# Layer A attention of a decoder trunk: the TensorE order written out, keys transposed two blocks later, the stages of a unit two and four steps apart, and the query root on POOL

## The chip, the cores and the metric

The kernel runs on one core of one Trainium2 chip. The metric is the device time of one execution in microseconds. The kernel before took 2514.96 us (median of 3 runs, 2512.82 to 2516.09). The engines are named as in the profile: PE is TensorE (matmuls and transposes), DVE is VectorE, ACT is ScalarE, POOL is GpSimd, SP is SyncE, which here issues DMAs. Each engine takes its own instructions strictly in the order in which they stand in its queue.

## The reference

The program is a trunk of four sub-layer pairs on x of 1024 rows by 1024 columns: layer A, a feed-forward block, layer B (stick-breaking attention), a feed-forward block. The change touches layer A alone, which computes

```
qkv = h @ w_qkv                              # h: normed, scaled and shifted x
q = rope(rmsnorm(q, q_gain)); k = rope(rmsnorm(k, k_gain))   # per head of 64
# 16 query heads in 2 groups of 8, one key/value head for each group
# for each block of 128 queries: keys of its own and of the block before
s = q @ k.T * 64 ** -0.5                      # 0 <= query - key < 128
p = softmax(concat(s, sink))[..., :-1]        # one sink logit for each head
x = x + gate * ((p @ v) @ w_o)
```

The rope turns only the first 16 of a head's 64 columns. The sums must come out in full fp32, while TensorE's fast format (fp32r) rounds its operands. So an operand is split into a rounded high part and a low part, the rest, and a product is made of three matmuls: high by high, high by low and low by high.

## The kernel before

The rows are cut into 8 blocks of 128. First `keys_values(b)` makes keys and values of block b: 24 matmuls of 256 columns (3 for each of 8 slices of the sum), a copy to `kvf` by ACT, the root of two heads (`head_rms`), gain and rope on POOL, the high and low part side by side in `kd`, and then four transposes of `kd` on PE (L461) and their copy into `KTs` (L462). The input norm comes in two halves of four blocks: `norm_half` (L474) turns the second half into `hth` and `htl`, the high and low part of h, between the keys of block 3 and of block 4.

Then come 16 units (g, b): head group g of 8 query heads, block b. A unit has three stages.

- `stage1`: the query projection, 24 matmuls of 512 columns into one PSUM bank `psd`; its product with the gain, `qn` (DVE, L490); the squares `sq` (ACT, L407), their sum (DVE, L409) and the root of 8 heads by three Newton steps, 12 small DVE instructions (L416 to L422); the rope on POOL, five small instructions (L430 to L434); the high part of `qs` (ACT, L495) and its low part (POOL, L496).
- `stage2`: 8 transposes of `qs` (PE, L505) in two halves, each copied into `QT` (ACT, L506); four times 4 matmuls of 256 columns, the scores `psz`, whose diagonal blocks ACT copies into `sm` (L520) and whose other half DVE puts in above the diagonal (L524); the maximum `mx` and the bias `nmx` (DVE, L525 to L532); 8 exponentials, one for each head (ACT, L535); the sum, its reciprocal and the product `sm` (DVE, L536 to L538).
- `stage3`, for each half of the heads: 4 transposes of `sm`, its high part `ph` (ACT, L548) and low part `pl` (DVE, L119); two selections `ow` of them on POOL (L559); 4 matmuls of 512 columns into the bank `psa` with the values; the copy `ob` (ACT, L563) and its DMA to DRAM.

The loop (L581 to L602) goes through steps t and traces `stage2` of unit t-1, `stage3` of unit t-3 and `stage1` of unit t, so the text of a step holds three units. Beside them stand weight work (the query weights of group 1, loaded at t = 8, with a high part on ACT and a low part on DVE; the output weights `W`, from t = 12 on), one `ada_step` a step (a slice of the next scale and shift row, DVE L268, and at t = 9 eight matmuls with `ones` and two with `diag`, L297, that make the gate row `grow`, L302), and behind the loop the output projection, which reads the units back from DRAM.

A tile scheduler orders the instructions of each engine by its own estimate of when they are ready. `chained` (L99 to L105) can tie each matmul to the one traced before it, so that TensorE's order becomes the written one; before the change this is off in layer A.

Of the kernel before, what the change touches and what calls it, by code (L numbers as in the profile page):

```python
# [18 lines left out]
P = 128  # L19
# [45 lines left out]
def build(tc, x_in, c_in, pos_in, ada_w, ada_b, n1g, n2g, wqkv_a, qn_a, kn_a, sinks, wo_a,  # L65
# [338 lines left out]
    def head_rms(src, nh, pool):  # L404
# [34 lines left out]
    def keys_values(b):  # L439
# [14 lines left out]
        kd = kt.tile([P, 2, 2, 2, HD], F32R, tag="kd", name=nm("kd"), bufs=2)  # L454
# [3 lines left out]
        pt = bank("t", F32R)  # L458
        kdf = kd.rearrange("p v e u d -> p (v e) (u d)")
        for j in range(4):  # L460
            chained(nc.tensor.transpose(pt[:, j * P : (j + 1) * P], kdf[:, j], identr))  # L461
        nc.scalar.copy(KTs[:, :, b * P : (b + 1) * P], pt.rearrange("p (j t) -> p j t", t=P))  # L462
# [20 lines left out]
    def stage1(g, b, wq):  # L483
        pb = bank("d")
        for k in range(KT):
            h, l = hA_blk(b, k)
            wh, wl = wq[k // 2]
            mm3(pb, h, l, wh[:, k % 2], wl[:, k % 2], k == 0, k == KT - 1)
# [5 lines left out]
        qs = wk.tile([P, 8, 2, HD], F32R, tag="qs", name=nm("qs"), bufs=2)  # L494
# [4 lines left out]
    def stage2(g, b, qs, r):  # L499
        QT = wk.tile([P, 8, P], F32R, tag="QT", name=nm("QT"), bufs=2)  # L500
        qsf = qs.rearrange("p h e d -> p h (e d)")
        for j in range(2):
            pt = bank("t", F32R)
            for h in range(4):
                chained(nc.tensor.transpose(pt[:, h * P : (h + 1) * P], qsf[:, 4 * j + h], identr))  # L505
            nc.scalar.copy(QT[:, 4 * j : 4 * j + 4], pt.rearrange("p (h t) -> p h t", t=P))  # L506
        sm = wk.tile([P, 8, P], F32, tag="sm", name=nm("sm"), bufs=3)
# [4 lines left out]
        for j in range(4):  # L512
# [26 lines left out]
        return sm  # L539

    def stage3(g, b, sm):
        for j in range(2):
# [6 lines left out]
            sub(pl, pt, ph)  # L549
            av = bank("a")  # L550
# [31 lines left out]
    for t in range(len(units) + 3):  # L582
# [5 lines left out]
        if t < len(units):  # L588
            g, b = units[t]
            if b == 0:  # L590
                with tc.issue_after(last_norm.ins):
                    wq[g] = load_q(g)
# [639 lines left out]
```

## Time and profile before

| | |
|---|---|
| median of 3 runs | 2514.96 us (2512.82 to 2516.09) |
| the profiled execution, its own time | 2506.01 us |
| its span in the profile | 2504.3 us |
| mean granted TensorE clock | 0.976 of full speed |
| busy: PE / DVE / ACT / POOL | 2359.5 / 1604.8 / 1036.6 / 646.4 us |

The span is the time from the first to the last instruction of the profiled execution. A granted clock of 1.00 is TensorE's 2.4 GHz level, and a stretch in which the mean lies between 0.5 and 1.00 was spent partly at the 1.2 GHz level. Busy time is the share in which an engine had work in hand. A TensorE row's duration is the time that one instruction takes from start to end; since matmuls are pipelined, what one costs in a dense stream is the distance of two starts.

### The profile page before, as it was taken

To read this page: it belongs to the slowest core of one execution; us is meant where nothing else is said; L and a number is where in the kernel's file an instruction comes from. 1 tells how busy PE (TensorE), PEld (TensorE's weight loads), DVE (VectorE), ACT (ScalarE), POOL (GpSimd) and SP (SyncE) were. 2 spreads that over 40 slices of the span, in tenths; PEclk is the share of its full clock that TensorE was granted. 3 is DMA by queue.
4 is the path that set the end of the run, shared out by engine and by line. 5 is a ranking of instruction groups with operands and counts; after the bars stand their busy time and mean duration, and the time that the engine had idled before them with its cause. 6 is when DMAs were issued, how large, how long until landed. Compare 5 with 4: busy or idle time off the path is not lost.

```text
span 2504.3 us, 31440 instructions
## 1 busy us (share of the span) xinstructions
PE 2359.5 (94%) x11404; PEld 1934.1 (77%) x11404; DVE 1604.8 (64%) x2319; ACT 1036.6 (41%) x2029; POOL 646.4 (26%) x671
## 2 busy tenths in 40 slices
PE   6899899799999999999999999988979999999999
PEld 5677677578787878887788888777758888887887
DVE  7679955765767677536677676696375454557553
ACT  4487723423232332104666666573343333323110
POOL 2344512223232300001444444341212322310000
PEclk9799899899999999999999999999989999999999
DMA  8113398143536264203222222127522222227211
GB/s 288 51 50 120 110 228 249 62 130 122 175 120 182 95 238 143 82 9 101 70 58 60 60 56 53 41 80 168 143 76 74 82 93 68 91 86 257 84 51 68
DMA packets 187195, 273.78 MB, mean 109 GB/s; under 512 B 11792, under 2 KB 131744, under 8 KB 187040
## 3 DMA queue, kind: packets, MB, share of 16 engines
q1 hardware_dynamic: 186416, 271.63, 35.2%
q8 instruction: 90, 1.47, 0.2%
q14 instruction: 65, 0.53, 0.1%
q10 hardware_dynamic: 624, 0.14, 0.0%
HBM read 206.72 MB, written 56.62 MB: 105 GB/s over the span
## 4 chain that ended last, share of the span: by engine, by line
PE 70%; DVE 9%; DMA 4%; issue 2%; ACT 2%; POOL 1%; SPq 0%; DVEq 0%; ACTq 0%; POOLq 0%
PE psz L108 24%; PE psd L108 21%; PE pst L108 16%; PE psa L108 5%; DMA ada<-in_ada_w_dram 2%; PE pst L116 2%; DVE nb L1101 2%; DVE acc L268 1%; DVE al L119 1%; DVE lT L119 1%; DVE Wl L309 0%; DMA wr<-in_wo_b_dram 0%; DVE QK L119 0%; DVE sl L631 0%; ACT nb L1094 0%
## 5 line engine op out<-in xcount | busy, mean ns | idle before, releaser
L630 ACT CAST sh<-rg 128x512 fp32r<-128x512 f32 x308 | 191.5, 622 | 565.6 <-PE psz L108 246.1
L631 DVE TENSOR_TENSOR sl<-rg,sh 128x512 fp32r<-128x512 f32 x308 | 244.8, 795 | 94.0 <-ACT sh L630 94.0
L108 PE MATMUL psd<-hth,whl 128*128 128x512 f32 x768 | 304.3, 415 | 0.1
L1103 POOL TENSOR_TENSOR bb<-bb,nb 128x895 f32<-128x895 f32 (+7 forms) x128 | 179.1, 1402 | 248.7 <-DVE nb L1101 159.5
L1101 DVE TENSOR_TENSOR_SCAN nb<-nb,ones 128x896 f32<-128x896 f32 (+7 forms) x128 | 192.4, 1508 | 44.3 <-ACT nb L1094 41.9
L308 ACT CAST dh<-raw 128x1024 fp32r<-128x1024 f32 x88 | 87.9, 1048 | 277.8 <-PE psa L108 174.9
L803 POOL TENSOR_TENSOR rg<-rg,rg 128x512 f32<-128x512 f32 x44 | 58.3, 1324 | 459.8 <-DMA rg<-in_w_up_dram 361.0
L108 PEld LDWEIGHTS psd<-hth,whl 128*128 128x128 f32 x768 | 146.5, 191 | 22.2 <-issue 1.3
L108 PE MATMUL psz<-hT,sh 128*128 128x512 f32 x352 | 139.5, 399 | 19.0 <-ACT hT L684 10.8
L108 PE MATMUL psd<-htl,whl 128*128 128x512 f32 x384 | 152.3, 399 | 1.8 <-DVE htl L119 1.6
L119 DVE TENSOR_TENSOR al<-pst,ah 128x512 fp32r<-128x512 f32 x160 | 108.3, 684 | 62.1 <-ACT ah L1124 59.5
L108 PE MATMUL psz<-lT,sh 128*128 128x512 f32 x352 | 140.0, 398 | 2.7 <-DVE lT L119 2.7
L108 PE MATMUL psz<-hT,sl 128*128 128x512 f32 x352 | 139.0, 395 | 0.0
L108 PE MATMUL psd<-hB,sl 128*128 128x512 f32 x352 | 137.4, 390 | 0.0
L108 PE MATMUL psd<-hB,sh 128*128 128x512 f32 x352 | 137.3, 390 | 0.0
L108 PE MATMUL psd<-lB,sh 128*128 128x512 f32 x352 | 137.0, 389 | 0.0
L268 DVE SCALAR_TENSOR_TENSOR acc<-ada,condT,acc 128x1024 f32<-128x1024 f32 x77 | 111.0, 1441 | 25.5 <-DMA ada<-in_ada_w_dram 24.8
L1094 ACT ACTIVATE nb<-psz 128x448 f32<-128x448 f32 (+3 forms) x192 | 95.3, 496 | 65.6 <-PE psz L108 61.3
L1124 ACT CAST ah<-pst 128x512 fp32r<-128x512 f32 x160 | 94.2, 591 | 54.1 <-PE pst L116 51.8
L309 DVE TENSOR_TENSOR dl<-raw,dh 128x1024 fp32r<-128x1024 f32 x88 | 104.6, 1220 | 9.8 <-ACT dh L308 9.8
L108 PE MATMUL psz<-QK,QK 128*128 128x384 f32 (+4 forms) x384 | 104.7, 356 | 2.5 <-ACT bb L1095 2.4
L108 PE MATMUL psa<-al,V 128*128 128x256 f32 x320 | 88.9, 299 | 17.5 <-DVE al L119 16.7
(325 smaller groups left out, 6336.8 us busy)
## 6 DMA issues: line engine op xcount, KB each, us to landing
ada<-in_ada_w_dram SPq DMA_DIRECT2D x96, 512.0 KB, 4.6
rg<-in_w_gate_dram SPq DMA_DIRECT2D x44, 512.0 KB, 3.6
rg<-in_w_up_dram SPq DMA_DIRECT2D x44, 512.0 KB, 5.7
raw<-hid SPq DMA_DIRECT2D x44, 512.0 KB, 6.6
raw<-in_w_down_dram SPq DMA_DIRECT2D x44, 512.0 KB, 4.4
hid<-f SPq DMA_DIRECT2D x64, 256.0 KB, 2.1
wr<-in_wqkv_b_dram SPq DMA_DIRECT2D x24, 512.0 KB, 4.2
odA<-ob SPq DMA_DIRECT2D x32, 256.0 KB, 2.5
```

The source lines that it names most:

```text
L108: chained(nc.tensor.matmul(o, l, r, start=start, stop=stop, skip_group_check=more))
L119: return nc.vector.tensor_tensor(o, a, h.bitcast(F32), op=ALU.subtract)
L268: i = nc.vector.scalar_tensor_tensor(a, wt, condT[:, j : j + 1], a, op0=ALU.mult, op1=ALU.add)
L308: nc.scalar.copy(h, raw)
L309: (eng or nc.vector).tensor_tensor(l, raw, h.bitcast(F32), op=ALU.subtract)
L630: nc.scalar.copy(hv, src)
L631: nc.vector.tensor_tensor(lv, src, hv.bitcast(F32), op=ALU.subtract)
L803: nc.gpsimd.tensor_tensor(A[1, 0], A[1, 0], A[1, 1], op=ALU.add)
L1094: nc.scalar.activation(nb[:, s0 : s0 + e], pz[:, 0:e], AF.Sigmoid, scale=-1.0)
L1101: nc.vector.tensor_tensor_scan(rv, rv, ones[:, 0:1].to_broadcast([P, L]), initial=1.0, op0=ALU.mult, op1=ALU.mult)
L1103: nc.gpsimd.tensor_tensor(bb[:, 0 : L - 1], bb[:, 0 : L - 1], nb[:, 1:L], op=ALU.mult)
L1124: nc.scalar.copy(ah_, pt)
```

## The change

- `head_rms` makes the root of 8 heads as it did that of 2: an addition and a power on POOL in place of the 12 small DVE instructions.
- `keys_values` no longer transposes. `keys_turned(b)` does, two blocks later, and `kd` has three buffers.
- TensorE's order is the traced one from the keys and values of block 0 up to the last query projection (`pe["on"]`).
- The first two query projections stand right behind the keys of block 7. From t = 2 on, a step weaves three streams of TensorE work: the projection of unit t in 8 parts, `stage2` of unit t-2 in 6 parts and `stage3` of unit t-4 in 4 parts. The rest of `stage1` (gain, root, rope, `qs`) is traced at the end of the step. `qs` has three buffers.
- In `stage3` both halves are transposed and split first, and the selections `ow` of a half are issued ahead of the matmuls of the half before. `ob` is written over `sm`, in place of a tile of its own.

```diff
@@ head_rms
-        if nh <= 2:
-            nc.gpsimd.tensor_scalar(r, r, EPS, None, op0=ALU.add)
-            nc.gpsimd.tensor_tensor(r, r, mhalf[:, 0:nh], op=ALU.pow)
-        else:
...
-            nc.vector.tensor_scalar(v, r, EPS, None, op0=ALU.add)
-            nc.vector.tensor_scalar(r.bitcast(I32), v.bitcast(I32), 1, None, op0=ALU.logical_shift_right)
-            nc.vector.tensor_scalar(r.bitcast(I32), r.bitcast(I32), -1, 0x5F3759DF, op0=ALU.mult, op1=ALU.add)
-            for _ in range(3):
-                nc.vector.tensor_tensor(t, r, r, op=ALU.mult)
-                nc.vector.scalar_tensor_tensor(t, v, -0.5, t, op0=ALU.mult, op1=ALU.mult)
-                nc.vector.scalar_tensor_tensor(r, t, 1.5, r, op0=ALU.add, op1=ALU.mult)
+        nc.gpsimd.tensor_scalar(r, r, EPS, None, op0=ALU.add)
+        nc.gpsimd.tensor_tensor(r, r, mhalf[:, 0:nh], op=ALU.pow)
@@ keys_values
-        kd = kt.tile([P, 2, 2, 2, HD], F32R, tag="kd", name=nm("kd"), bufs=2)
+        kd = kt.tile([P, 2, 2, 2, HD], F32R, tag="kd", name=nm("kd"), bufs=3)
...
+    def keys_turned(b, kd):
+        pt = bank("t", F32R)
+        kdf = kd.rearrange("p v e u d -> p (v e) (u d)")
+        for j in range(4):
+            chained(nc.tensor.transpose(pt[:, j * P : (j + 1) * P], kdf[:, j], identr))
+        nc.scalar.copy(KTs[:, :, b * P : (b + 1) * P], pt.rearrange("p (j t) -> p j t", t=P))
...
+    def proj_q(g, b, wq):
+        pb = bank("d")
+        q_banks[g, b] = pb
+        for k in range(KT):
+            h, l = hA_blk(b, k)
+            wh, wl = wq[k // 2]
+            mm3(pb, h, l, wh[:, k % 2], wl[:, k % 2], k == 0, k == KT - 1)
+            yield
+    pe["on"] = True
     for b in range(4):
-        keys_values(b)
-    norm_half(xta, xA, 0, adaT[:, 0, 0], *HA[1], True)
+        kd[b] = keys_values(b)
+        if b >= 2:
+            keys_turned(b - 2, kd[b - 2])
+    xns = norm_rows(xta, xA, True)
+    for kk in range(KT):
+        norm_cols(xns, kk, xA, 0, adaT[:, 0, 0], *HA[1])
+        if kk in (3, 7):
+            b = 2 + kk // 4
+            keys_turned(b, kd[b])
+    with tc.issue_after(last_norm.ins):
+        wq[0] = load_q(0)
     for b in range(4, NB):
-        keys_values(b)
+        kd[b] = keys_values(b)
+        if b >= 6:
+            keys_turned(b - 2, kd[b - 2])
+    for b in range(2):
+        for _ in proj_q(0, b, wq[0]):
+            pass
+        keys_turned(6 + b, kd[6 + b])
+    pe["on"] = False
@@ stage1
-        qs = wk.tile([P, 8, 2, HD], F32R, tag="qs", name=nm("qs"), bufs=2)
+        qs = wk.tile([P, 8, 2, HD], F32R, tag="qs", name=nm("qs"), bufs=3)
@@ stage3
+            parts.append((ph, pl))
+            yield
...
+        ows = rest(0)
+        for j, (ph, pl) in enumerate(parts):
             av = bank("a")
...
+            if j == 0:
+                ows = rest(1)
-            ob = wk.tile([P, 512], F32, tag="ob", name=nm("ob"), bufs=2)
+            ob = sm[:, 4 * j : 4 * j + 4].rearrange("p h t -> p (h t)")
             nc.scalar.copy(ob, av)
...
+    def weave(parts):
+        todo = sorted(((i + 0.5) / n, j) for j, (_, n) in enumerate(parts) for i in range(n))
+        for _, j in todo:
+            next(parts[j][0], None)
...
-    for t in range(len(units) + 3):
+    for t in range(n + 4):
...
-        if 1 <= t <= len(units):
-            s2[units[t - 1]] = stage2(*units[t - 1], *s1.pop(units[t - 1]))
-        if t >= 3:
-            stage3(*units[t - 3], s2.pop(units[t - 3]))
-        if t < len(units):
-            s1[units[t]] = stage1(g, b, wq[g])
+        pe["on"] = t < n
+        parts = []
+        if 2 <= t < n:
+            parts.append((proj_q(*units[t], wq[units[t][0]]), KT))
+        if 2 <= t < n + 2:
+            parts.append((stage2(*units[t - 2], *s1.pop(units[t - 2])), 6))
+        if t >= 4:
+            parts.append((stage3(*units[t - 4], s2.pop(units[t - 4])), 4))
+        weave(parts)
+        if t < n:
+            s1[units[t]] = stage1(*units[t])
         if t >= 2 and len(ada_list) > 8:
             ada_some(1)
             if len(ada_list) == 16:
                 row_a = grow_make(0, 0)
+    pe["on"] = False
```


The next rows are ACT's queue in the kernel before, in a step of the first head group (`ph` and `ob` are of one unit, `sm` of the exponentials of the next, `qs` and `sq` of a third).

```order
L548 CAST ph_321_1760<-pst_320_1755 128x512
L548 CAST ph_328_1781<-pst_327_1776 128x512
L520 COPY sm_311_1706<-psz_316_1729 128x256
L407 ACTIVATE sq_336_1824<-psd_334_1797 128x512
L495 CAST qs_342_1849<-qn_335_1822 128x8x64
L563 COPY ob_326_1773<-psa_323_1764 128x512
L506 COPY QT_344_1855<-pst_345_1856 128x512
L535 ACTIVATE sm_311_1706,su_319_1739<-sm_311_1706,nmx_317_1737,rs_301_1664 128x128
L533 ACTIVATE se_318_1738<-se_318_1738 128x8
L535 ACTIVATE sm_311_1706,su_319_1739<-sm_311_1706,nmx_317_1737,rs_301_1664 128x128 x7
L563 COPY ob_333_1794<-psa_330_1785 128x512
```

And these are ACT's rows of such a step after the change, from the squares of one projection to the second high part.

```order
L407 ACTIVATE sq_296_1656<-psd_270_1527 128x512
L526 COPY QT_303_1679<-pst_304_1680 128x512
L514 CAST qs_300_1669<-qn_295_1654 128x8x64
L574 CAST ph_306_1691<-pst_305_1686 128x512
L526 COPY QT_303_1679<-pst_308_1698 128x512
L556 ACTIVATE se_293_1634<-se_293_1634 128x8
L558 ACTIVATE sm_280_1568,su_294_1635<-sm_280_1568,nmx_292_1633,rs_237_1374 128x128 x8
L574 CAST ph_310_1712<-pst_309_1707 128x512
L541 COPY sm_312_1716<-psz_314_1718 128x256
```

Before, both `ph` stood ahead of `qs` and ahead of the exponentials that follow it; now the first stands behind `qs`, then comes the second copy into `QT`, then the eight exponentials, and the second `ph` behind them.

The next rows are DVE's queue in the same step of the kernel before.

```order
L490 TENSOR_TENSOR qn_335_1822<-psd_334_1797,qg_93 128x512
L536 TENSOR_TENSOR su_283_1577<-su_283_1577,se_282_1576 128x8
L537 RECIPROCAL su_283_1577<-su_283_1577 128x8
L524 COPY_PREDICATED sm_311_1706<-up_89,psz_313_1708 128x256
L538 TENSOR_TENSOR sm_275_1544<-sm_275_1544,su_283_1577 128x1024
L524 COPY_PREDICATED sm_311_1706<-up_89,psz_314_1715 128x256
L524 COPY_PREDICATED sm_311_1706<-up_89,psz_315_1722 128x256
L524 COPY_PREDICATED sm_311_1706<-up_89,psz_316_1729 128x256
L119 TENSOR_TENSOR pl_322_1761<-pst_320_1755,ph_321_1760 128x512
L525 TENSOR_REDUCE mx_312_1707<-sm_311_1706 128x8
L119 TENSOR_TENSOR pl_329_1782<-pst_327_1776,ph_328_1781 128x512
```

And these are DVE's rows in such a step after the change.

```order
L509 TENSOR_TENSOR qn_295_1654<-psd_270_1527,qg_93 128x512
L548 TENSOR_REDUCE mx_281_1569<-sm_280_1568 128x8
L409 TENSOR_REDUCE rs_297_1658<-sq_296_1656 128x8
L553 SCALAR_TENSOR_TENSOR nmx_292_1633<-mx_281_1569,rs_237_1374 128x8
L554 TENSOR_TENSOR nmx_292_1633<-nmx_292_1633,nsink_143 128x8
L555 TENSOR_TENSOR se_293_1634<-sink_95,nmx_292_1633 128x8
L119 TENSOR_TENSOR pl_307_1692<-pst_305_1686,ph_306_1691 128x512
L559 TENSOR_TENSOR su_294_1635<-su_294_1635,se_293_1634 128x8
L560 RECIPROCAL su_294_1635<-su_294_1635 128x8
L561 TENSOR_TENSOR sm_280_1568<-sm_280_1568,su_294_1635 128x1024
L119 TENSOR_TENSOR pl_311_1713<-pst_309_1707,ph_310_1712 128x512
L545 COPY_PREDICATED sm_312_1716<-up_89,psz_314_1718 128x256
```

Before, the second `pl` (`pl_329`) stood behind the product of exponentials (`sm_275`, L538) that stand ahead of `qs_342` on ACT; now the second `pl` (`pl_311`) stands right behind the product of exponentials (`sm_280`, L561) that stand behind `qs_300` on ACT. The Newton rows (L416 to L422), which end just above the rows of before, are gone.

The next rows are TensorE's queue before, where the second unit's value matmuls (`psa`) stand.

```order
L108 MATMUL psz_316_1729<-KTs_490,QT_308_1693 128x256 x4
L108 MATMUL psa_323_1764<-ph_321_1760,VA_491 128x512
L108 MATMUL psd_370_1959<-wl_180_1073,hth1_9_157 128x512
L108 MATMUL psd_370_1959<-wh_179_1072,htl1_10_158 128x512
L108 MATMUL psd_370_1959<-wh_182_1078,hth1_9_157 128x512
L108 MATMUL psd_370_1959<-wl_183_1079,hth1_9_157 128x512
L108 MATMUL psd_370_1959<-wh_182_1078,htl1_10_158 128x512
L108 MATMUL psd_370_1959<-wh_182_1078,hth1_9_157 128x512
L108 MATMUL psd_370_1959<-wl_183_1079,hth1_9_157 128x512
L108 MATMUL psd_370_1959<-wh_182_1078,htl1_10_158 128x512
L108 MATMUL psd_370_1959<-wh_185_1084,hth1_9_157 128x512
L108 MATMUL psd_370_1959<-wl_186_1085,hth1_9_157 128x512
```

And these are TensorE's rows at the end of a step after the change (`psa_322` is the second half of `stage3`, `psd_302` the projection of the step).

```order
L108 MATMUL psz_321_1756<-KTs_490,QT_303_1679 128x256 x4
L108 MATMUL psd_302_1675<-wh_145_848,hth1_9_157 128x512
L108 MATMUL psd_302_1675<-wl_146_849,hth1_9_157 128x512
L108 MATMUL psd_302_1675<-wh_145_848,htl1_10_158 128x512
L108 MATMUL psa_322_1766<-ph_310_1712,VA_491 128x512
L108 MATMUL psa_322_1766<-pl_311_1713,VA_491 128x512
L108 MATMUL psa_322_1766<-ow_319_1747,DV_492 128x512
L108 MATMUL psa_322_1766<-ow_320_1749,DV_492 128x512
L108 MATMUL psz_323_1773<-KTs_490,QT_303_1679 128x256 x4
L108 MATMUL psd_302_1675<-wh_145_848,hth1_9_157 128x512
L108 MATMUL psd_302_1675<-wl_146_849,hth1_9_157 128x512
L108 MATMUL psd_302_1675<-wh_145_848,htl1_10_158 128x512
```

Before, the value matmuls stood among the first matmuls of the next unit's projection (`psd_370`), behind the end of `psd_334`. Now the second half's four stand ahead of the step's last scores and of the last three matmuls of its projection.

## Rows read from the trace of the kernel before

**Rows 1.** The page: span, and busy time of each engine.
```profile
span 2504.3 us, 31440 instructions
...
PE 2359.5 (94%) x11404; PEld 1934.1 (77%) x11404; DVE 1604.8 (64%) x2319; ACT 1036.6 (41%) x2029; POOL 646.4 (26%) x671
```

**Rows 2.** Busy time by stretch: stretch, length, PE, PEld, DVE, ACT, POOL (instructions), PEclk, DMA, GB/s.
```profile
68.00:113.00 45.00, 35.19 (x183) 28.18 (x181) 28.24 (x61) 17.88 (x41) 19.52 (x56) 0.84 0.20 59
113.00:189.00 76.00, 71.80 (x390) 60.08 (x391) 55.95 (x171) 57.60 (x177) 29.54 (x51) 0.93 0.12 42
189.00:300.00 111.00, 98.56 (x516) 78.44 (x514) 102.82 (x240) 82.65 (x242) 55.28 (x76) 0.94 0.38 124
```

**Rows 3.** Timeline of ACT: start, duration, work; projections 1, 2, 7 and 15 ending.
```profile
112.56 0.59 ACT L407 ACTIVATE sq<-psd 128x512 f32<-128x512 f32 x1
...
129.30 0.58 ACT L407 ACTIVATE sq<-psd 128x512 f32<-128x512 f32 x1
...
189.16 0.61 ACT L407 ACTIVATE sq<-psd 128x512 f32<-128x512 f32 x1
189.64 0.64 ACT L495 CAST qs<-qn 128x512 fp32r<-128x512 f32 x1
...
300.19 0.60 ACT L407 ACTIVATE sq<-psd 128x512 f32<-128x512 f32 x1
```

**Rows 4.** Groups by line and form, 113 to 324 us: busy us, mean ns, idle before.
```profile
L535 ACT ACTIVATE sm<-sm,nmx,rs 128x128 f32<-128x128 f32 x128 | 61.6, 486 | 5.9 <-DVE nmx L531 5.9
...
L538 DVE TENSOR_TENSOR sm<-sm,su 128x1024 f32<-128x1024 f32 x16 | 20.5, 1283 | 0.3
L119 DVE TENSOR_TENSOR pl<-pst,ph 128x512 fp32r<-128x512 f32 x30 | 20.2, 680 | 0.8 <-POOL ow L559 0.8
...
L559 POOL TENSOR_SCALAR_AFFINE_SELECT ow<-pl 128x512 fp32r<-128x512 f32 x26 | 18.6, 714 | 10.5 <-DVE nmx L530 4.4 <-DVE pl L119 3.6 <-DVE rt L420 0.8
...
L505 PE MATMUL pst<-identr,qs 128*128 128x128 f32 x128 | 17.1, 257 | 7.7 <-POOL qs L496 7.7
...
L490 DVE TENSOR_TENSOR qn<-psd,qg 128x512 f32<-128x512 f32 x14 | 9.6, 687 | 10.9 <-PE psd L108 10.9
L420 DVE TENSOR_TENSOR rt<-rs 128x8 f32<-128x8 f32 x47 | 9.4, 201 | 1.1
...
L308 ACT CAST wh<-wr 128x1024 fp32r<-128x1024 f32 x4 | 4.2, 1072 | 0.0
...
L297 DVE TENSOR_TENSOR diag<-ident,adaT 128x1024 f32<-128x1024 f32 x1 | 1.2, 1225 | 0.0
```

**Rows 5.** Timeline of PE: two matmuls of one projection, and one unit's eight transposes.
```profile
80.06 0.40 PE L108 MATMUL psd<-wl,hth 128*128 128x512 f32 x1
80.30 0.39 PE L108 MATMUL psd<-wh,htl 128*128 128x512 f32 x1
...
132.29 0.87 PE L505 MATMUL pst<-identr,qs 128*128 128x128 f32 x8 [1.05 <-POOL qs L496]
```

**Rows 6.** Timeline of all engines: first exponential, rope, sum behind the exponentials, `qs`.
```profile
125.10 0.49 ACT L535 ACTIVATE sm<-sm,nmx,rs 128x128 f32<-128x128 f32 x1
...
128.26 0.32 POOL L430 TENSOR_TENSOR ra<-qn,cs 128x64 f32<-128x64 f32 x1 [13.79 <-DVE qn L490]
...
129.17 0.28 DVE L536 TENSOR_TENSOR su<-su,se 128x8 f32<-128x8 f32 x1 [0.99 <-ACT sm L535]
...
130.00 0.62 ACT L495 CAST qs<-qn 128x512 fp32r<-128x512 f32 x1
```

**Rows 7.** Timeline of DVE: the last low part of the input norm.
```profile
88.40 0.69 DVE L119 TENSOR_TENSOR htl<-nt,hth 128x512 fp32r<-128x512 f32 x1
```

**Rows 8.** Instructions of L412, the power on POOL: min/median/max ns.
```profile
L412 POOL TENSOR_TENSOR rs<-rs,mhalf x8: 708/708/715, 57.5 to 104.2; 128x2 f32<-128x2 f32 x8
```

**Rows 9.** Timelines of PE and DVE: the first output projection matmul, and its next operand.
```profile
324.15 0.42 PE L108 MATMUL psd<-Wh,rg 128*128 128x512 f32 x1
...
325.47 1.23 DVE L649 TENSOR_TENSOR rg<-rg,rg 128x1024 fp32r<-128x1024 f32 x1
```

More of the change, by code (lines that the diff above doesn't have):

```diff
@@ L457, in keys_values @@
         sub(kd[:, :, 1], knb, kd[:, :, 0])
[L458 to L462, printed above, removed]
         if b < NB - 1:
@@ L471, in keys_values, with load_q @@
         vlast[b] = vf
-    for b in range(4):
-        keys_values(b)
-    norm_half(xta, xA, 0, adaT[:, 0, 0], *HA[1], True)
-    for b in range(4, NB):
-        keys_values(b)
+        return kd
+    def keys_turned(b, kd):
[4 more added lines that the diff above has]
+        nc.scalar.copy(KTs[:, :, b * P : (b + 1) * P], pt.rearrange("p (j t) -> p j t", t=P))
+    def load_q(g):
+        return [load_k(wa[2 * P * j : 2 * P * (j + 1)], slice(512 * g, 512 * g + 512)) for j in range(4)]
+    def proj_q(g, b, wq):
[6 more added lines that the diff above has]
+            yield
+    q_banks, wq, kd = {}, {}, {}
+    pe["on"] = True
+    for b in range(4):
+        kd[b] = keys_values(b)
[9 more added lines that the diff above has]
+        wq[0] = load_q(0)
+    for b in range(4, NB):
+        kd[b] = keys_values(b)
[6 more added lines that the diff above has]
+    pe["on"] = False
     pools.close(cm_kt)
@@ L481, in build, with stage1 @@
     cm_wa, wk = pools.open("wkA", "left")
[L483 to L488, printed above, removed]
+    def stage1(g, b):
+        pb = q_banks.pop((g, b))
         q3 = wk.tile([P, 8, HD], F32, tag="qn", name=nm("qn"), bufs=2)
@@ L524, in stage2 @@
                 nc.vector.copy_predicated(so, upb, z3[:, :, 0:P])
+            if j < 3:
+                yield
         nc.vector.tensor_reduce(mx, sm, axis=AX.X, op=ALU.max)
@@ L538, in stage2 @@
         nc.vector.tensor_tensor(sm, sm, su[:, :, None].to_broadcast([P, 8, P]), op=ALU.mult)
-        return sm
+        s2[g, b] = sm
+        yield
     def stage3(g, b, sm):
+        parts = []
         for j in range(2):
@@ L549, in stage3, with rest @@
             sub(pl, pt, ph)
+            parts.append((ph, pl))
+            yield
+        def rest(j):
+            ows = []
+            for i, src in enumerate(parts[j] if b else ()):
+                ow = wk.tile([P, 512], F32R, tag=f"ow{i}", name=nm("ow"), bufs=1)
+                nc.gpsimd.affine_select(ow.rearrange("p (h n) -> p h n", n=P), src.rearrange("p (h n) -> p h n", n=P),
+                                        [[0, 4], [1, P]], ALU.is_ge, 0.0, base=0, channel_multiplier=-1)
+                ows.append(ow)
+            return ows
+        ows = rest(0)
+        for j, (ph, pl) in enumerate(parts):
             av = bank("a")
@@ L572, in ada_some @@
                 ada_step(*ada_list.pop(0))
-    def load_q(g):
-        return [load_k(wa[2 * P * j : 2 * P * (j + 1)], slice(512 * g, 512 * g + 512)) for j in range(4)]
     units = [(g, b) for g in range(2) for b in range(NB)]
     s1, s2 = {}, {}
-    wq = {}
     row_a = None
     W = []
-    for t in range(len(units) + 3):
+    n = len(units)
+    for t in range(n + 4):
         if t >= 12:
@@ L587, in build @@
                 load_o(W, wo_a[0], k, row_a, wp, "wr")
-        if t < len(units):
[L589 to L592, printed above, removed]
-        if 1 <= t <= len(units):
-            s2[units[t - 1]] = stage2(*units[t - 1], *s1.pop(units[t - 1]))
-        if t >= 3:
-            stage3(*units[t - 3], s2.pop(units[t - 3]))
-        if t < len(units):
-            s1[units[t]] = stage1(g, b, wq[g])
+        if t < n and units[t][1] == 0 and t:
+            wq[1] = load_q(1)
+        pe["on"] = t < n
+        parts = []
+        if 2 <= t < n:
[7 more added lines that the diff above has]
+            s1[units[t]] = stage1(*units[t])
         if t >= 2 and len(ada_list) > 8:
```

8 lines of the change are left out of this document (2 added, 6 removed).

## Prediction

> **What bounds the kernel now.** I read the page first: PE is busy for 94% of the span [rows 1], so a change can gain only where PE waits or runs at the lower clock. Then the stretches. Layer A attention is the part from 68 to about 324 us. PE is idle there for 45.00 - 35.19 = 9.8 us before 113, 76.00 - 71.80 = 4.2 us from 113 to 189 and 111.00 - 98.56 = 12.4 us from 189 to 300 [rows 2], and the granted clock is 0.84, 0.93 and 0.94. The timeline of ACT dates the ends of the projections by their squares: unit 1 at 112.56, unit 2 at 129.30, unit 7 at 189.16, unit 15 at 300.19 [rows 3]. So a step took 16.74 us from unit 1 to 2, (189.16 - 129.30) / 5 = 11.97 us up to unit 7, and (300.19 - 189.16) / 8 = 13.88 us from there, where DVE is busy for 102.82 of 111.00 us, 93% [rows 2], with the weight work. From unit 2 to unit 15 it is 170.89 us, 13 steps.
>
> What PE needs for a step: two matmuls of 512 columns start 0.24 us apart (80.06, 80.30) and 8 transposes take 0.87 us [rows 5]. A step has 24 such matmuls in the projection and 8 in the values, 16 transposes, and 16 score matmuls of 256 columns, at half of 0.24 by their columns (an estimate from the same rows): 32 x 0.235 + 2 x 0.87 + 16 x 0.12 = 11.2 us. The clean steps of 11.97 us are thus nearly all PE. Behind 330 us both kernels have the same order, and I give the rest no change.
>
> **The Newton root.** Of the 12 DVE instructions those of L420 take 201 ns each [rows 4]; 12 x 0.20 = 2.4 us a unit go. What comes is an addition and a power on POOL. The power takes 0.708 us for two columns [rows 8]; for 8 columns no row shows it. It lies between 0.7 us (no growth) and 4 x 0.708 = 2.8 us (all of it by columns); I take 1.5 us, between them. POOL is busy for 55.28 of 111.00 us [rows 2], so 2.8 us more in a step of 13 us fits, and nothing waits for the root before the unit's `nmx`, a step later. In the clean steps DVE is busy for 55.95 of 76.00 us and 2.4 us less gains nothing; in the loaded ones it does, and the sum below has it.
> By the Trainium skill, page "Perfetto Trace Analysis", section "Optimizing Scalar/DVE Operations", DVE and GPSIMD share a read port of SBUF, so that moving work between them might not help. By that rule the three steps with output weights would stay at 13.9 us in place of the 13.5 below, 1.2 us more; no row shows a power of 8 columns beside DVE's work.
>
> **The new loop.** The three streams of a step now hang on each other through four queues. After the order shown with the change, I follow one step from the end of a projection to the end of the next:
> - `qn` on DVE, 0.69 us [rows 4];
> - the rope on POOL: starts at 128.26, and `qs` starts on ACT behind it at 130.00, 1.74 us [rows 6];
> - ACT in order: `qs`, the first `ph`, the second copy of `QT`. Such instructions of 512 columns start 0.48 us apart (189.16, 189.64) [rows 3]: 1.45 us;
> - the eight exponentials, which stand behind these on ACT: from 125.10 to the sum on DVE at 129.17, 4.07 us [rows 6];
> - sum and reciprocal, 0.5 us (two instructions like those of L420 with their handoff), and the product `sm`, 1.28 us [rows 4], of which 1.13 us are its distance to the next;
> - `pl` of the second half, 0.68 us, and the selection `ow` of it on POOL, 0.71 us [rows 4];
> - PE: the last value matmul, 4 scores and the last three projection matmuls, which stand behind that `ow`: 0.24 + 4 x 0.12 + 3 x 0.24 = 1.4 us [rows 5].
>
> That is 0.69 + 1.74 + 1.45 + 4.07 + 0.5 + 1.13 + 0.68 + 0.71 + 1.4 = 12.4 us, and twelve handoffs between engines at 0.03 to 0.1 us make it 13.1 us. Before, the exponentials of a step were ahead of `qs` and PE ran on into the projection after, so the same chain came back two projections later and had twice the time. So a clean step takes 13.1 us where PE needs 11.2: PE would wait some 1.9 us in each.
>
> Step by step, by the unit whose projection ends it: units 3 and 4, where the streams fill, 12.2 and 12.1; units 5, 6, 9, 11 and 15 at 13.1 = 65.5; unit 7 13.7 with the first load of weights; unit 8 15.2, as four high parts of 1.07 us [rows 4] enter ACT's queue, of which some half fits the loop's slack on ACT; unit 10 18.9, as the eight matmuls with `ones` and the two with `diag` now stand in PE's written order and PE waits for DVE's `diag`, 1.23 us [rows 4], and the copies around it, where before it could go on; units 12 to 14 at 13.5 = 40.5, DVE's share of 13.88 less what is left of the 2.4 us beside the loop. Sum 12.2 + 12.1 + 65.5 + 13.7 + 15.2 + 18.9 + 40.5 = 178.1 us against 170.9: 7.2 us more.
>
> **The front.** The last low part of the input norm ends at 88.40 + 0.69 = 89.09 [rows 7], and the change does not touch what makes it. Behind it PE has the keys of blocks 5 to 7 and an eighth of block 4, 3.1 x 24 x 0.12 = 8.9 us, two projections, 48 x 0.235 = 11.3 us, and some five sets of four key transposes, 2.2 us: 111.5 us at full clock. Before, the second projection ends at 112.56. I take no change; ends -1.5 us (no wait at all) and +5 us (ten us at the lower clock, as the mean of 0.84 has it for 14 of 45 us in this stretch [rows 2]).
>
> **The first step.** Unit 1 to unit 2 took 16.74 us, with PE waiting for `qs` (7.7 us in all for L505, [rows 4]). Now the first two `qs` are both under way when the loop starts. On POOL the rope of unit 1 stands ahead of the low part of unit 0, so the transposes start some 4.0 us after projection 1 ends, and then 6.8 us of the projection's matmuls and the scores follow that could not go ahead: 10.8 us, 5.9 less; ends 10 and 14 us.
>
> **The tail.** From the end of the last projection to the first output matmul it was 324.15 - 300.19 = 24.0 us, and the operand `rg` of the next block started at 325.47 [rows 9]. Now two units are still to be scored when the projections are done, not one, and one more set of exponentials (4.07 us) stands on ACT, of which I count 3 us as seen; ends 0 and 6 us.
>
> **Sum.** 0 - 5.9 + 7.2 + 3 = +4.3 us. The profiled execution took 2506.01 us, so 2510.3 on its scale; the median is 8.95 us above the profiled one, so I predict 2514.96 + 4.3 = 2519.3, given as 2519. Two tenths of a per cent, about what a measurement of this kernel tells from no change, are 5 us; the forecast lies at that edge.
>
> **Rivals.**
> A, the loop does not bind. If the exponentials start earlier than I read (when `mx` is late it costs nothing, and when POOL's rope is quicker ACT starts sooner) or the handoffs are hidden, PE sets the pace: 13 steps at 12.0 us, the clean pace of before, plus 4 us for unit 10, 160 us, 10.9 less. With -5.9 and +3 that is 2514.96 - 13.8 = 2501. For it: DVE loses 2.4 us where it was 93% busy, and PE's 16.6 us of waiting in the 13 steps are there to be had. Against it: each link of the loop has a row.
> B, the waits cost clock. PE would stand still once a step at the same place. In the trace the granted clock is lowest where PE waits most: 0.84 in the stretch with 22% idle, 0.93 where 6% are idle [rows 2]. If in each step the part of the loop on PE (1.4 us) and its handoffs run at the 1.2 GHz level, a step gets 1.5 us longer, 13 x 1.5 = 20 us: 2539. It decides from a mean clock below some 0.85 in the steps. Against it: 0.94 was granted from 189 to 300 us, where PE waited 11%, little less than the 1.9 of 13.1 us that I forecast.
> By the Trainium skill, page "TensorE: Matmul & The Clock Gate", section "What's actually happening", the throttled clock is the default and activity releases it, so by that page waits regular enough would give this time.
> C, gains and losses cancel: the loop takes 12.8 us in place of 13.1, and 2515 comes out.
>
> **How the numbers follow.** The loop as forecast 45%, with a range of its own of 2511 to 2530 (the ends of front, first step and tail, and 0.4 us more or less a step); A 30%; B 13%; C 12%. Faster by over 0.2%, below 2510: A nearly whole, and a little of C, 0.32. Within 0.2%, up to 2520: C, and some half of the loop, 0.32. Slower: the other half of the loop and B, 0.36. Eight in ten reach from 2498 to 2540, which leaves out the outer half of A's lower side and of B.
>
> **What would show it.** Right: the squares 13 us apart in the clean steps, PE waiting some 2 us a step for POOL's `ow` or DVE's `pl`, the exponentials starting right behind the second `QT` copy, the first step near 11 us, a step of 18 to 19 us at unit 10. Wrong: squares 11 to 12 us apart with PE idle below 5%, which is A; a clock below 0.85 in the steps, which is B; or a first projection that ends later than 116 us, which would break the front's term.

## The result, and the profile after

The kernel after took 2525.39 us (median of 6 runs, 2524.26 to 2534.26) against 2513.81 us before (now a median of 6 runs too): 1.0051 times as long, interval [1.0037, 1.0066], 11.6 us slower. The forecast was 2519 us, 4.3 us slower.

The page of the kernel after, to be read beside [rows 1]:

```profile
span 2525.5 us, 31295 instructions
...
PE 2358.9 (93%) x11404; PEld 1931.9 (76%) x11404; DVE 1583.6 (63%) x2127; ACT 1037.9 (41%) x2029; POOL 669.4 (27%) x703
```

DVE has 21 us less to do and POOL 23 us more; PE is busy for as long and waits more. The same stretches as in [rows 2], with the same columns:

```profile
68.00:113.00 45.00, 36.16 (x212) 32.27 (x211) 25.11 (x54) 16.13 (x39) 16.71 (x51) 0.83 0.21 59
113.00:189.00 76.00, 65.87 (x358) 51.33 (x356) 40.16 (x82) 53.07 (x155) 42.45 (x63) 0.98 0.07 26
189.00:300.00 111.00, 91.82 (x504) 71.74 (x502) 84.15 (x136) 78.96 (x232) 63.98 (x90) 0.98 0.38 120
```

From 189 to 300 us DVE fell from 93% to 76%, and PE is idle for 19.2 us in place of 12.4; from 113 to 189 for 10.1 us in place of 4.2. The clock rose from 0.93 and 0.94 to 0.98. The squares of units 1, 2, 7 and 15 by ACT's timeline, beside [rows 3]:

```profile
116.10 0.59 ACT L407 ACTIVATE sq<-psd 128x512 f32<-128x512 f32 x1
...
126.87 0.60 ACT L407 ACTIVATE sq<-psd 128x512 f32<-128x512 f32 x1 [1.22 <-DVE qn L509]
...
189.89 0.60 ACT L407 ACTIVATE sq<-psd 128x512 f32<-128x512 f32 x1
...
307.01 0.58 ACT L407 ACTIVATE sq<-psd 128x512 f32<-128x512 f32 x1
```

The first step takes 10.8 us, the next 13 take 180.1. The first profile of before was a short execution: its own time lies 8 us below the median. So the kernel before was run once more, unchanged:

> The kernel before once more, for a second profile of it: its profiled execution of 2506 us lies 8 us below its median, so stages of its trace could be short by chance. Expected: the ends of the projections within 1 us of the first profile (unit 15 at 300.2), the 8 us behind 330 us; rival: they are in the attention.

It took 2514.29 us, and the same rows (unit 7 left out) are

```profile
113.90 0.59 ACT L407 ACTIVATE sq<-psd 128x512 f32<-128x512 f32 x1
...
130.60 0.59 ACT L407 ACTIVATE sq<-psd 128x512 f32<-128x512 f32 x1
...
301.86 0.62 ACT L407 ACTIVATE sq<-psd 128x512 f32<-128x512 f32 x1
```

Both profiles have 16.7 us for the first step, and 170.9 and 171.3 us for the 13 others. Unit 15's squares come 1.7 us later and not within 1 us; 1.3 us of it come from ahead of unit 1's, and the rest of the 8 us lies behind 324 us, as expected. Cut at the squares, the stages are, in us, with the differences against the first and the second profile of before:

| stage | before, first | before, second | after | differences | forecast |
|---|---|---|---|---|---|
| front, to unit 1's squares | 112.6 | 113.9 | 116.1 | +3.5, +2.2 | 0 |
| first step, to unit 2's | 16.7 | 16.7 | 10.8 | -6.0, -5.9 | -5.9 |
| 13 steps, to unit 15's | 170.9 | 171.3 | 180.1 | +9.3, +8.9 | +7.2 |
| tail, to the last residual of the output projection | 134.2 | 137.1 | 139.8 | +5.7, +2.8 | +3 |
| sum of these | | | | +12.5, +7.9 | +4.3 |

The medians are 11.6 us apart, which lies between the two sums. Behind the last residual the program is the same, and 14 profiles of all the kernels here spread there over 10 us, from 2070.0 us (the kernel before) to 2080.0 (e4); the kernel after has 2078.6. So from single profiles that stretch tells nothing of the change.

The squares are not the end of a projection. `qn` on DVE waits for its last matmul, and unit 1's and unit 15's are, before and then after:

```profile
109.18 0.69 DVE L490 TENSOR_TENSOR qn<-psd,qg 128x512 f32<-128x512 f32 x1 [0.71 <-PE psd L108]
...
283.72 0.69 DVE L490 TENSOR_TENSOR qn<-psd,qg 128x512 f32<-128x512 f32 x1 [0.27 <-PE psd L108]
```

```profile
113.09 0.69 DVE L509 TENSOR_TENSOR qn<-psd,qg 128x512 f32<-128x512 f32 x1 [2.24 <-PE psd L108]
...
305.40 0.67 DVE L509 TENSOR_TENSOR qn<-psd,qg 128x512 f32<-128x512 f32 x1
```

Before, PE was done with projection 15 some 16 us ahead of its squares at 300.19, which stand late in ACT's queue; after, 1.6 us ahead. The sum does not depend on where it is cut, but the stages do: cut at `qn`, the first step goes from 18.3 to 13.0 us.

A clean step of the kernel after is 12.90 us. The profile's chain of waits of one (start, duration, what), from `qn` to the next `qn`:

```profile
149.78 0.69 DVE qn L509
...
152.28 0.62 ACT qs L514
152.90 0.48 ACT ph L574
153.39 0.50 ACT QT L526
...
153.93 0.65 PE pst L116 x4
...
159.97 0.92 PE psa L108 x3
...
161.45 0.59 ACT sm L602
...
162.69 0.70 DVE qn L509
```

The head is the forecast one: `qn`, rope, `qs`, first `ph`, second copy into `QT`, 4.1 us. Behind it this view follows PE, whose next transposes wait for that copy's bank. But PE's row of work has gaps at its end. The leg that the forecast named stands beside it, in the timeline of the same step, where PEld is the load of a matmul's stationary operand, which runs beside the matmul ahead of it:

```profile
153.87 0.49 ACT L558 ACTIVATE sm<-sm,nmx,rs 128x128 f32<-128x128 f32 x1
153.93 0.65 PE L116 MATMUL pst<-ident,sm 128*128 128x128 f32 x4 [0.94 <-ACT QT L526]
...
154.65 0.64 POOL L583 TENSOR_SCALAR_AFFINE_SELECT ow<-ph 128x512 fp32r<-128x512 f32 x1
...
157.83 0.17 DVE L559 TENSOR_TENSOR su<-su,se 128x8 f32<-128x8 f32 x1 [3.72 <-ACT sm L558]
...
158.27 1.22 DVE L561 TENSOR_TENSOR sm<-sm,su 128x1024 f32<-128x1024 f32 x1
158.33 1.65 POOL L583 TENSOR_SCALAR_AFFINE_SELECT ow<-ph 128x512 fp32r<-128x512 f32 x1 [0.80 <-ACT ph L574]
...
159.41 0.68 DVE L119 TENSOR_TENSOR pl<-pst,ph 128x512 fp32r<-128x512 f32 x1
...
159.81 0.40 PE L108 MATMUL psa<-ph,VA 128*128 128x512 f32 x1
...
160.15 0.19 PEld L108 LDWEIGHTS psa<-pl,VA 128*128 128x128 f32 x1 [0.38 <-DVE pl L119]
...
160.23 0.63 POOL L583 TENSOR_SCALAR_AFFINE_SELECT ow<-pl 128x512 fp32r<-128x512 f32 x1 [0.24 <-PE psa L108]
...
160.91 0.19 PEld L108 LDWEIGHTS psa<-ow,DV 128*128 128x128 f32 x1 [0.47 <-POOL ow L583]
...
161.25 0.63 PE L108 MATMUL psz<-KTs,QT 128*128 128x256 f32 x4
```

The last `ow` is ready at 160.86, and the load that waits for it starts at 160.91. The half's first matmul started at 159.81; with the forecast's 0.235 us for each of its four, the scores behind them would start at 160.75 and not at 161.25. So PE's own leg is some 0.5 us the shorter (an estimate), and the forecast leg ends last. By these rows its links, from `qn` over rope, ACT's three, exponentials, sum and reciprocal, product, `pl` and `ow` to the next `qn`, took 2.50, 1.59, 3.96, 0.44, 1.14, 0.82, 0.68 and 1.78 us, 12.91 in all; the forecast has 2.43, 1.45, 4.07, 0.5, 1.13, 0.68, 0.71 and 1.4, with some 0.7 for handoffs.

### The profile page after: what moved, and what is told of

Same layout as the page of the kernel before. It is cut to its first block, busy times and chain, and to the rows that moved or that the text cites. A ratio compares the mean times of both kernels' runs of the same rounds, so it can differ in the third digit from the quotient of the medians.

```text
span 2525.5 us, 31295 instructions
## 1 busy us (share of the span) xinstructions
PE 2358.9 (93%) x11404; PEld 1931.9 (76%) x11404; DVE 1583.6 (63%) x2127; ACT 1037.9 (41%) x2029; POOL 669.4 (27%) x703
## 4 chain that ended last, share of the span: by engine, by line
PE 73%; DVE 12%; DMA 5%; ACT 5%; issue 2%; POOL 2%; SPq 0%; ACTq 0%; DVEq 0%; POOLq 0%
PE psz L108 25%; PE psd L108 23%; PE pst L108 17%; PE psa L108 6%; PE pst L116 3%; DMA ada<-in_ada_w_dram 2%; DVE nb L1147 2%; DVE acc L268 2%; DVE al L119 1%; ACT sm L558 1%; DMA rg<-odA 1%; DMA xsp<-xt 1%; DVE lT L119 1%; DVE Wl L309 1%; DMA wr<-in_wqkv_b_dram 1%
## 5 line engine op out<-in xcount | busy, mean ns | idle before, releaser
L677 DVE TENSOR_TENSOR sl<-rg,sh 128x512 fp32r<-128x512 f32 x308 | 232.4, 755 | 95.0 <-ACT sh L676 94.8
L268 DVE SCALAR_TENSOR_TENSOR acc<-ada,condT,acc 128x1024 f32<-128x1024 f32 x77 | 117.0, 1520 | 29.8 <-DMA ada<-in_ada_w_dram 28.9
```

The costliest lines, as they stand in the source:

```text
L268: i = nc.vector.scalar_tensor_tensor(a, wt, condT[:, j : j + 1], a, op0=ALU.mult, op1=ALU.add)
L677: nc.vector.tensor_tensor(lv, src, hv.bitcast(F32), op=ALU.subtract)
```

## The experiments

The experiments are timed in 5 rounds against the kernel before on the same chip. "Clean step" is the distance of two `qn`, the mean from unit 4 to unit 6. In e7 and e11 the steps are unequal (8.8 to 16.5 us by the squares), and the table has the mean of the six steps from unit 1 to 7 by the squares; by that measure the kernel after has 12.3.

| run | ratio to before | interval | clean step, us |
|---|---|---|---|
| kernel after | 1.0051 | [1.0037, 1.0066] | 12.9 |
| e1_qs_behind_QT | 1.0010 | [1.0001, 1.0018] | 12.4 |
| e2_pl_before_exp | 1.0037 | [1.0023, 1.0051] | 12.9 |
| e3_both | 1.0054 | [1.0042, 1.0066] | 12.4 |
| e4_gate_free | 1.0049 | [1.0035, 1.0062] | 12.9 |
| e5_newton_on_DVE | 1.0072 | [1.0054, 1.0091] | 12.9 |
| e6_before_pow | 1.0009 | [0.9999, 1.0020] | as before |
| e7_no_written_order | 0.9997 | [0.9986, 1.0007] | (11.6) |
| e8_exp_split | 1.0015 | [1.0005, 1.0025] | 12.6 |
| e9_values_later | 1.0024 | [1.0016, 1.0033] | 12.8 |
| e10_values_later_qs_behind | 0.9987 | [0.9977, 0.9996] | 11.8 |
| e11_no_order_at_all | 0.9970 | [0.9958, 0.9982] | (11.4) |

**e1, e2, e3: which leg binds.** For these, `split_q` holds the two `qs` lines of `stage1`, and `soft` holds the exponentials, sum and product of `stage2`; both are called in the middle of the next step. `behind(i, k)` puts i, on its engine, behind the instruction last noted under k, without a semaphore.

```diff
@@ e1
+    FIRST, FIRST_V = ['qs'], []
+            s1[units[t - 1]] = split_q(*s1[units[t - 1]])
+            behind(at["qs"], "QT")
+            soft(*units[t - 3])
@@ e2
+    FIRST, FIRST_V = ['ph'], ['pl']
+            soft(*units[t - 3])
@@ e3
+    FIRST, FIRST_V = ['ph'], ['pl']
+            soft(*units[t - 3])
+            s1[units[t - 1]] = split_q(*s1[units[t - 1]])
+            behind(at["qs"], "ex")
```

> The kernel after, with one thing moved on ACT: the high part of qs stands behind the second copy into QT, so the order is squares, QT, first ph, QT, qs, exponentials, second ph. Theory two legs: a step of the kernel after (12.90 us, 162.69 to 175.59) is the chain qn, rope, qs, first ph, second QT copy (4.1 us), and from there two legs of equal length to the last value matmul (7.0 us), one of PE's own work in its written order and one of exponentials, product, pl and ow. Here PE's leg no longer waits for the rope and the other starts 0.96 us earlier, so clean steps come to 11.9 to 12.0 us and the time to about 8 to 12 us below the kernel after. Theory of the prediction (only the leg by the exponentials binds): the same here. Rival (POOL and DVE hold each other up, or PE's own pace): steps stay at 12.9 us and the time within 3 us.

> The kernel after, with the second ph ahead of the exponentials on ACT and the second pl ahead of the sum and the product on DVE; qs and the QT copies stay where they were. The leg exponentials, product, pl, ow no longer leads to the last value matmul of the step; PE's own leg behind the second QT copy stays. Theory two legs: clean steps stay at 12.7 to 12.9 us, the time within 3 us of the kernel after. Theory of the prediction: only that leg binds, so steps fall to 12 us or less, some 10 to 15 us off the time. Rival (contention or PE's pace): no change.

> The kernel after with both: the second ph and pl ahead of the exponentials and the product, and the high part of qs behind the exponentials, so that neither leg passes the rope. Theory two legs: PE sets the pace, clean steps 11.2 to 11.8 us, the time 12 to 20 us below the kernel after (2505 to 2513 us). Theory of the prediction: as much. Rival (contention or PE's pace): steps stay at 12.9 us.

These expectations speak of two legs of equal length; by the rows above, PE's own is the shorter. e1 fell to 1.0010, some 10 us off the kernel after by the ratios: the head with the rope matters. Its steps came to 12.4 us and not to 11.9. The rope is off the path there, and the exponentials are still on it: PE's values wait for `pl`.

```profile
PE psa L108 <- DVE pl L119: 0.6, 2, 0.3
```

e2 left the step at 12.9 us. But it did not take the exponentials off the path either. There is one bank for `psa`, and ACT empties it with `ob` (L563 before, L624 here), which stands behind the exponentials; the second half's values wait for that:

```profile
161.35 0.19 PEld L108 LDWEIGHTS psa<-ph,VA 128*128 128x128 f32 x1 [0.71 <-ACT sm L624]
```

So e2 does not show that PE's own leg holds the step; it shows that the exponentials come back to PE by a second way. e3 opened both legs and stopped at 12.4 us, with nothing gained in the whole time. The same second way holds it, longer by the `qs` copy, which now stands between the exponentials and `ob` (L627):

```profile
174.13 0.50 PE L108 MATMUL psa<-ph,VA 128*128 128x512 f32 x1 [1.06 <-ACT sm L627]
```

```profile
171.99 0.48 ACT L580 ACTIVATE sm<-sm,nmx,rs 128x128 f32<-128x128 f32 x1
...
172.46 0.60 ACT L526 CAST qs<-qn 128x512 fp32r<-128x512 f32 x1
...
173.50 0.58 ACT L627 COPY sm<-psa 128x512 f32<-128x512 f32 x1
```

**e8: the way over `ob` opened.** The exponentials are parted, so that `ob` need not wait for all eight.

```diff
+            if h == 5:
+                yield
...
+            if h >= 5:
+                behind(i, "ob")
+                behind(i, "so")
...
+        parts.append((middle(t), [0.4, 0.7]))
```

> As e3_both, and the exponentials parted in two on ACT: five, then the copy of a score block and the copy ob of the first half, then three, and behind them the high part of qs. In e3_both a third leg bound the step (12.43 us): PE's second half of the values waits 1.06 us for the one bank of psa, whose copy ob stood behind all eight exponentials and qs. Theory: that wait goes and PE sets the pace, clean steps 11.3 to 11.6 us, the time 10 to 15 us below e3_both. Rival (steps of 12.4 us are PE's own pace with its handoffs): no change in the clean steps, the time within 3 us of e3_both.

The time came down by some 10 us, as expected (1.0054 to 1.0015), but the clean steps stayed at 12.6 us, as the rival had it: PE now waits for `qs`, which came later still, behind all eight exponentials. The group of PE's waits from 149 to 176 us (us in total, times, longest):

```profile
PE pst L537 <- POOL qs L527: 2.7, 3, 1.4
```

Where the time was saved I can only date: by the squares e8 is 1.6 us ahead of e3 at unit 1, 1.9 at unit 7, 4.3 at unit 10 and 10.6 at unit 15.

**e4: the gate row.** The ten matmuls are taken out of the written order.

```diff
+            held, pe["on"], pe["prev"] = dict(pe), False, None
             ada_some(1)
...
+            pe.update(held)
```

> The kernel after, with the eight matmuls with ones and the two with diag (the gate row) left out of TensorE's written order, so that the scheduler places them. Theory: the step of unit 10 takes 21.5 us since PE stands in its written order until DVE's diag is there and the second diag matmul's bank is free; freed, it falls to 15 to 17 us and the time by 4 to 6 us. Rival (that step is bound by DVE and ACT, with the new scale row and the output weights' casts): it stays above 20 us, the time within 2 us.

The squares of units 8, 9 and 10, first of e4 and then of the kernel after:

```profile
205.21 0.60 ACT L407 ACTIVATE sq<-psd 128x512 f32<-128x512 f32 x1 [1.15 <-DVE qn L509]
223.12 0.60 ACT L407 ACTIVATE sq<-psd 128x512 f32<-128x512 f32 x1 [0.57 <-DVE qn L509]
239.60 0.60 ACT L407 ACTIVATE sq<-psd 128x512 f32<-128x512 f32 x1 [0.21 <-DVE qn L509]
```

```profile
205.43 0.60 ACT L407 ACTIVATE sq<-psd 128x512 f32<-128x512 f32 x1 [1.15 <-DVE qn L509]
218.33 0.60 ACT L407 ACTIVATE sq<-psd 128x512 f32<-128x512 f32 x1 [1.15 <-DVE qn L509]
239.79 0.60 ACT L407 ACTIVATE sq<-psd 128x512 f32<-128x512 f32 x1 [3.04 <-DVE qn L509]
```

34.4 us for the two steps either way. The step of unit 10 alone fell to 16.5 us, but the one ahead of it rose from 12.9 to 17.9. So the written order is not what costs the time here, as the rival had it. The rival's own cause, the load of DVE and ACT, is not shown: neither was busy throughout (DVE 24.7 and ACT 20.1 of the 34.4 us in the kernel after).

**e5, e6: the root.** e5 puts the `if nh <= 2` and the Newton lines back into the kernel after; e6 takes them out of the kernel before.

```diff
@@ e6, and e5 the other way round
-        if nh <= 2:
...
+        nc.gpsimd.tensor_scalar(r, r, EPS, None, op0=ALU.add)
+        nc.gpsimd.tensor_tensor(r, r, mhalf[:, 0:nh], op=ALU.pow)
```

> The kernel after with one part undone: the root of 8 heads by the 12 DVE instructions again in place of the two on POOL. Theory: the root lies on no leg of the clean steps, which stay at 12.9 us; in the steps with weight work and in the tail DVE gets 2.4 us a unit back, so the time rises by 3 to 12 us over the kernel after. Rival (the power on POOL, 1.67 us and up to 2.7, holds up ow and qs and is what makes the kernel after slow): the time falls by 3 us or more.

> The kernel before with one part of the change alone: the root of 8 heads on POOL. Theory: DVE was busy for 93% of 189 to 300 us there, so that stretch shortens and the time falls by 4 to 12 us. Rival (the port that DVE and POOL share, or the rope and qs waiting behind the power on POOL): no gain, within 3 us, or slower.

In the kernel after the root on POOL is worth 0.2% at most (1.0072 against 1.0051, intervals that overlap, so it is not shown); the clean steps don't see it. In the kernel before it brought nothing (1.0009), though DVE's 93% fell to 77%: the outcome is the rival's, and which of its two causes it was is not shown. The first output matmul came earlier there, at 321.5 us for 324.2 and 326.0 in the two profiles of before, but the last residual did not, at 440.7 for 434.4 and 438.9: what the attention gained was lost in the output projection.

**e7, e11: the written order taken out,** in the loop, and then in the keys' part too.

```diff
@@ e7
-        pe["on"] = t < n
+        pe["on"] = False
@@ e11, besides
     q_banks, wq, kd = {}, {}, {}
-    pe["on"] = True
+    pe["on"] = False
```

> The kernel after with TensorE's order left to the scheduler from the first weave on (the keys' part keeps its written order); stages two and four steps apart as after. Theory (the loop through ACT's and DVE's queues sets the step, not TensorE's written order): clean steps stay at 12.4 to 13 us and the time within 5 us of the kernel after. Rival (the written order is what makes PE wait): clean steps fall to 12.0 us or less, the time by 8 us or more.

> e7_no_written_order with the keys' part, too, left to the scheduler: of the change only the spacing of the stages, the keys transposed later in the program, the early projections and the root on POOL stay. Theory: the second projection ends at 112 to 114 us as before in place of 116.1 (by the squares) and the time falls 1 to 3 us below e7 (ratio to before 0.998 to 0.9995). Rival: the front's later squares come from the rope's and sq's places, not from the written order; no change against e7 (0.9997).

My expectation of e7 failed: 0.9997 and not 1.003 to 1.007, 13.6 us off the kernel after. Its squares of units 1 and 7:

```profile
116.72 0.59 ACT L407 ACTIVATE sq<-psd 128x512 f32<-128x512 f32 x1
...
186.30 0.62 ACT L407 ACTIVATE sq<-psd 128x512 f32<-128x512 f32 x1
```

The steps between them take 8.8, 8.9, 11.6, 11.6, 16.5 and 12.3 us. PE fills its waits with projection matmuls, and the second half's values stand behind the projection's end. e11 gains a further 0.27%, more than expected. There unit 1's squares start at

```profile
111.70 0.59 ACT L407 ACTIVATE sq<-psd 128x512 f32<-128x512 f32 x1
```

5 us before e7. The waits of PE from 43 to 113 us, first of the kernel after, whose front is e7's, then of e11:

```profile
PE pst L462 <- ACT kd L445: 9.3, 1, 9.3
PE pst L116 <- ACT KTs L463: 5.9, 1, 5.9
```

```profile
PE pst L462 <- ACT kd L445: 8.7, 5, 2.2
```

In the written order the transposes of block 0 stand ahead of the fourth block's matmuls and PE stands for 9.3 us at one place, and for 5.9 us at another, where the norm's transposes need the bank that ACT's copy into `KTs` empties. Unwritten, the waits for `kd` come in five pieces, that for `KTs` is gone, and PE does other work in between: the last `htl` is done at 88.4 us (91.2 in e7), and some 20 of the 48 matmuls of the first two projections start before that, while in the kernel after the first of them starts at 101.5. e11 is faster than the kernel before by 0.3%, the best of all.

**e9, e10: the order still written, but the values later.** The second half's value matmuls go into the next step, behind its first `QT` transposes. e9 holds ACT to the order of the kernel after; e10 adds e1.

```diff
+        if late is not None:
+            parts.append((late, [0.1]))
...
+            late = stage3(*units[t - 4], s2.pop(units[t - 4]))
+            parts.append((late, [0.125, 0.375, 0.625]))
```

> The kernel after with TensorE's order still written out, but the four value matmuls of the second half written behind the projection's end and the next step's first QT transposes, where the scheduler puts them in e7; on ACT only their copy ob moves, to behind qs. Theory (the written order closes the loop inside one step, since the second half's values stand ahead of the projection's last matmuls): the leg exponentials, product, pl, ow is open, PE's own leg is 1.2 us of value matmuls shorter and 0.5 us of ob longer, clean steps 11.8 to 12.3 us in place of 12.9, the time 6 to 12 us below the kernel after, ratio to before 1.000 to 1.003. Rival (a written order as such costs, wherever the values stand): clean steps stay at 12.7 us or more, ratio 1.004 to 1.006.

> e9_values_later and e1_qs_behind_QT together: values of the second half behind the projection's end, the high part of qs behind the second QT copy. Theory: no leg passes the rope or the exponentials within one step any more, PE sets the pace, clean steps 11.3 to 11.7 us, the time 12 to 18 us below the kernel after, ratio to before 0.998 to 1.000. Rival (the written order costs as such): no better than e1 (1.001) or e9.

e9 is half a hit: the time fell as expected (1.0024), the clean steps did not (12.7 and 12.8 us, as the rival had them). PE's waits from 138 to 176 us show the next leg, over the score copies that stand behind `pl` on DVE, and so again behind the exponentials:

```profile
PE psz L108 <- DVE sm L554: 3.1, 3, 1.3
```

e10 came out as expected in time, 0.9987, and nearly so in its steps: 11.8 us from unit 4 to 6, and 34.3 us for the three from unit 3, which took 37.8 in the kernel after. A written order can thus be as fast as the scheduler's in the loop, if it closes no leg within the step; its front still has the 5 us. Step by step the paths of e1, e2, e3, e8 and e9 are different, but each goes through the eight exponentials, some 4 us on ACT.

## Why the prediction was right or wrong

- **Clean steps**: right, in size and in mechanism: 12.90 us measured, 13.1 forecast, and the forecast chain through `qn`, rope, ACT's three, exponentials, `pl` and `ow` ends last, link by link as added up. PE's own leg behind the second `QT` copy ends some 0.5 us ahead of it. e1 shows that the head counts, and e10 against e1 that the end does (12.4 to 11.8 us when the values come later). e2, which opened the end alone, gained nothing, as the exponentials came back over `ob`. Steps near PE's own pace came only when both the `qs` copy and the values were moved (e10) or PE was left free (e7).
- **The front**: the term "I take no change" failed, and not by its sum. PE's work behind the last `htl` was forecast at 22.4 us at full clock, and from the end of the row below to `qn` at 113.09 it took 22.4, part of it at the lower clock. The sum was set against the wrong mark: 112.56, "the second projection ends", is the start of its squares, and the projection before had ended by 109.18, when `qn` starts. With that mark the same sum gives +2.3 us; measured at `qn` it is +3.9 and +2.6 against the two profiles of before. What the written order adds there, e11 against e7 shows: without it unit 1's `qn` starts at 108.6 us and not at 113.7. In the written order PE stands for 9.3 and 5.9 us and has done nothing of the projections when the last `htl` is there:

```profile
90.03 0.69 DVE L119 TENSOR_TENSOR htl<-nt,hth 128x512 fp32r<-128x512 f32 x1
```

- **The first step**: -5.9 us to the tenth by the squares, and that is in part luck. The forecast counted its 10.8 us from the end of projection 1; from there, at `qn`, it took 13.0, where it had taken 18.3 and not 16.7, so that the gain is 5.3 us.
- **The 13 steps**: +8.9 or +9.3 us for +7.2. The step of unit 10 took 21.5 us for 18.9, and not because PE waited for `diag` in the written order (e4).
- **The tail**: +2.8 or +5.7 us for +3, by which profile of before is taken; the two differ by as much as the whole term, so that the agreement is luck. At the points that the forecast named, against the second profile, it is +0.8 us (first output matmul) and +2.4 us (its next operand). That it comes from one more unit in flight is argued, not shown.
- **The root**: the power takes 1.88 us in the mean, 1.67 to 2.7, for the 1.5 taken, as POOL's group shows:

```profile
L411 POOL TENSOR_TENSOR rs<-rs,mhalf 128x8 f32<-128x8 f32 x16 | 30.1, 1883 | 0.7
```

 By the Trainium skill, page "Perfetto Trace Analysis", section "Optimizing Scalar/DVE Operations", GPSIMD and DVE share an SBUF read port, so that moving work between the two might not help. e6's time agrees with it (1.0009), e5's points the other way, but not clear of the noise, and no run shows the port as the cause.
- **Rivals**: A (the loop doesn't bind) is out by the clean steps, 12.9 us and not 12.0, and B (the waits cost clock) by the clock, 0.98. C's 2515 us is missed as well.
- **The sum**: +4.3 forecast, +7.9 or +12.5 up to the last residual, +11.6 by the medians. I had set the likeliest case at the edge of no change; the front's 2 to 4 us and the steps' 2 took it to the slower side.

## What to carry to other kernels

A written order of an engine that works far ahead takes away its way of filling waits: before writing one, follow every instruction that others wait for back to the last one it waits for, and see that no such chain closes within one step; a position one step later may cost nothing. When a chain is cut and the step does not move, look in the new trace for the way by which the same work comes back before giving up the theory, and try the change without its costliest part: here the change without the written order is 0.3% faster than before, and the order written over it costs 0.8%. And date a stage's end by an instruction that waits for it, not by one that stands in a queue behind others.

## What the runs showed of the hardware

- The granted clock rose to 0.98 from 113 to 300 us though PE was idle there for 13 and 17%, against 6 and 11% and 0.93 and 0.94 before. No wait of PE there is longer than 2.8 us; but before it was 2.3, so why the clock rose is not shown. In the long wait of 9.3 us for `kd`, from 53.4 to 62.7 us, and behind it TensorE was at the 1.2 GHz level, from 56.2 to 69.6 us (stretch, length, busy times as above, clock 0.50):

```profile
56.20:69.60 13.40, 5.85 (x28) 5.67 (x28) 7.53 (x19) 5.83 (x17) 9.25 (x23) 0.50 0.20 59
```

- A selection on POOL took 0.64 us alone and 1.65 us beside DVE's product `sm` (154.65, and 158.33 beside 158.27, above), so the second half's `ow` of `ph` is a microsecond late in these steps. It is not on the path: `ow` of `pl` waits for `pl`, which ends later.
